# Four quads in a layer's output projection, a shorter sum of weights, and a last norm shared by three engines

## The chip, the cores and the metric

The kernel runs on one core of a Trainium2 chip. The metric is the device time of one execution in microseconds (us); the time before is the median of 3 runs. The engines are named as the profile names them: TensorE (PE; its weight loads are PEld), VectorE (DVE), ScalarE (ACT), GpSimd (POOL) and SyncE (SP), which issues most DMA transfers.

## The reference

A decoder trunk of two layers over 256 tokens with 2048 features, in float32: attention with an output projection, a norm, a gated feed-forward network (FFN) with a short convolution, and a norm again. Cut to what the change touches (layer 2 has `layer == 1`):

```python
for layer in range(DEPTH):                       # 2 layers, x: (1, 256, 2048)
    attn = attention(h, ...)                     # 16 heads of 128; ends with  o @ w_o, (256, 2048) @ (2048, 2048)
    h = layer_norm(ALPHA * h + attn, ln_g[layer, 0], ln_b[layer, 0])
    ffn = conv_ffn(h, ...)                       # ends with  (gelu(g) * v) @ w_down, (256, 5504) @ (5504, 2048)
    h = layer_norm(ALPHA * h + ffn, ln_g[layer, 1], ln_b[layer, 1])

def layer_norm(x, g, b):
    mu, var = mean(x), mean(square(x - mu))
    return (x - mu) * rsqrt(var + 1e-5) * g + b
```

## The kernel before

All weights stream from HBM once, as "halves" of 128x1024 float32 (512 KB). SP loads a half into one of 7 raw buffers (`load_weights`, L115). ScalarE makes its high part, rounded to TensorE's fast float32r format (`high_upto`, L134), and VectorE the remainder (`low_piece`, L143), which frees the raw buffer for the load of the seventh half behind it. A product of a block of weights is three matmuls: high activations by high weights, high by low, low by high (L358 to L360, L566 to L568). The split halves lie in 4 rotating buffers, and, near the changes of stages, in spare "homes" in tiles that are free then (`aside`), with a longer look-ahead (`reach`, set by `settle`).

The order on every engine is written by hand. A call of `take` hands out the next half and records the splits of the halves up to three ahead (`AHEAD`), or as many as `reach` says. `step` ends a half; `at(n, f)` records work of other engines n halves later, `pe_at` that of TensorE.

The projections (`project_out`) have the tokens in two tiles of 128 (t = 0, 1) and the 2048 outputs in four chunks of 512 (c), each of which accumulates over all blocks k of 128 inputs in a bank of PSUM. There are 8 banks, 4 named `acc` and 4 named `at`. In the attention's projection (16 blocks, 32 halves) chunk after chunk is done, both tiles together; at the end of a chunk VectorE folds the bank into the residual `res` (`fold`, L459 or L452) and measures it (`measure`, L464). In the last chunk the last 16 blocks go tile by tile (`tilewise`): all of t = 0, then all of t = 1, so that the norm of the first tile (`moments`, `norm`, L586 to L598) and its transposes (`turn`, L607) run beside the second tile's matmuls. `load_gb` brings gamma and beta.

The FFN's down projection takes two chunks at once (`two_chunks`) and does most of it in "quads": two blocks k by two chunks c by two tiles t, 8 block products, are made with 7, by the Winograd form of Strassen's scheme. For that it needs sums of weights, and sums of activations (`sums`, `four_sums`, `split_sums`). The sums of weights are made in HBM long before their use, by SP's copies and POOL's accumulating DMAs (`sum_weights`, `plan_sums`), and are loaded as halves like the others. Of a quad's blocks 7 are streamed in place of 4. The sums of products are taken apart at the end (`chain`), with banks `a`, `s1`, `s2` and `s3` of kind `at`.

The last norm of the kernel, after layer 2's FFN, is on VectorE: for the second tile it folds the last chunk, measures, finds mean and deviation, and then goes over each of the four chunks twice (L597, L598), each followed by an output transfer on SP (L600).

Of the kernel before, what the change touches and what calls it, by code (L numbers as in the profile page):

```python
# [11 lines left out]
F32 = mybir.dt.float32  # L12
F32R = mybir.dt.float32r
# [30 lines left out]
WARM = 18  # L44
COLS = 2 * (((0, 4), (4, 8), (8, 12), (12, 16)),)
# [6 lines left out]
QUADS = ((10, 8), (10, 8))  # L52
DENSE = ((False, True), (False, False))
LEAD = (4, 2)
S_EARLY = 8
SUMS_AHEAD = (2, 2)
QUAD_ORDER = ((0, 1, 2, 3, 4, 5, 8, 9, 6, 7), (0, 1, 2, 3, 4, 5, 6, 7))
QUAD_LIST = [(l, n, p) for l in range(2) for n in range(2) for p in range(QUADS[l][n])]


def quad_halves(l, n):

    q = QUADS[l][n]
# [10 lines left out]
    return order + [two() for _ in range(len(plain) // 2)]  # L76

# [6 lines left out]
def trunk(ctx: ExitStack, tc: tile.TileContext, wst, wq, xT_in, x_in, relb, onehot, umask, sinks, conv_in, ln_g, ln_b, out):  # L84
# [13 lines left out]
    for l, width in enumerate((4 * D + 2 * DFF, 2 * KVH * P + 2 * D + 2 * DFF)):  # L98
        source += [wst[next(used)] for _ in range(width * D // (P * HW))]
        for n in range(2):  # L100
            source += [tsum[l, n, h[1]][h[2]] if h[0] == "t" else wst[next(used)] for h in quad_halves(l, n)]
# [159 lines left out]
    def sum_weights(q, i):  # L261
# [80 lines left out]
    class Moving:  # L342
# [12 lines left out]
        def mm(self, acc, k, t, wh, wl):  # L355
            sh = self.src(k)[:, t * P:(t + 1) * P]
            sl = self.src(k)[:, T + t * P:T + (t + 1) * P]
            nc.tensor.matmul(acc, sh, wh, start=(k == 0), stop=False)  # L358
# [3 lines left out]
        def tilewise(self, accs, k, n, done):  # L362
# [47 lines left out]

    def scale_shift():
        return [gbp.tile([P, D], F32, name=f"gb{i}") for i in range(2)]

    def project_out(src, nk, li, homes, preload, turnover=None, paired=None, early_sums=None):
# [5 lines left out]
        n_here = sum(len(quad_halves(li // 2, n)) for n in range(2)) if paired is not None else nk * NCH // 2  # L420
# [18 lines left out]
        stats = stat.tile([P, 2, NCH, 6], F32, name="stats", bufs=1, padded_shape=[P, 2, NCH, 10])  # L439
        l = li // 2  # L440
# [13 lines left out]
        ag, rs = {}, {}  # L454

        def fold(n, t, acc, first):
            z = res[:, t, n * 512:(n + 1) * 512]
            if first:
# [7 lines left out]
        def evac(n, t, acc):  # L466
            fold(n, t, acc, paired is None)
            measure(n, t)

        def sums(p):  # L470


            f = paired[:, 0:2 * T].rearrange("p (a b) -> p a b", b=T)

            def whole():
                for i in range(2):
# [595 lines left out]
```

## Time and profile before

| | |
|---|---|
| time, median of 3 runs | 2064.59 us (2064.36 to 2064.78) |
| the profiled execution: its time | 2064.55 us |
| its span, first to last instruction | 2062.8 us |
| granted clock of TensorE, mean | 0.998 |
| busy: TensorE, VectorE, ScalarE, POOL | 2048.8, 1547.9, 1055.3, 118.7 us |
| DMA | 518.37 MB, mean 251 GB/s |

Times in a timeline are from the start of the span. A line of a timeline has the start, the duration, the engine, the line of the kernel, the operation, what it writes and reads, the shape, and, in brackets, the idle time of the engine before it with what ended that. A line of a group has the number of instructions, their busy time and the mean of one in ns. A line of the windows has, for a stretch, the busy time of TensorE, its weight loads, VectorE, ScalarE and POOL, then the granted clock of TensorE, the DMA engines' busy share and what they moved in GB/s. A line of the transfers has their number, their size and the median time from issue to landing.

### The profile page before, as it was taken

The numbers are of one execution on the slowest core, as the hardware profiler recorded it, in microseconds if no ns is written. First come the engines' busy times: TensorE is split into PE (matmuls) and PEld (weight loads), VectorE is DVE, ScalarE is ACT, GpSimd is POOL, SyncE is SP. The second block draws the span as 40 slices with busy tenths as digits, with TensorE's granted clock in tenths as the row PEclk, the third lists the DMA queues.
The fourth block names the chain that finished last, engine by engine and source line by source line (L and its number), as shares of the span: only waits on it lengthen the run. The fifth ranks groups of instructions, "written<-read, shape, count | busy, mean of one in ns | idle before, by whom it ended". The sixth has DMA issues, their size and how long they took to land.

```text
span 2062.8 us, 29246 instructions
## 1 busy us (share of the span) xinstructions
PE 2048.8 (99%) x10968; PEld 1771.4 (86%) x10968; DVE 1547.9 (75%) x2295; ACT 1055.3 (51%) x1470; POOL 118.7 (6%) x130
## 2 busy tenths in 40 slices
PE   9999999999999999999999999999999999999997
PEld 7888888988888888888888888898888888888886
DVE  5555557698887878787786677688887787887767
ACT  5544446344545455565563555445454545556553
POOL 0000000001111111000000000001111111000000
PEclk9999999999999999999999999999999999999999
DMA  9666868379999998688894685639999999769883
GB/s 320 200 207 225 233 226 299 112 245 296 299 294 295 296 266 248 192 281 310 296 326 143 194 244 171 242 118 297 293 292 297 290 303 253 223 205 318 286 301 116
DMA packets 160830, 518.37 MB, mean 251 GB/s; under 512 B 18048, under 2 KB 22720, under 8 KB 159920
## 3 DMA queue, kind: packets, MB, share of 16 engines
q1 hardware_dynamic: 132176, 460.23, 63.1%
q0 software_dynamic: 28224, 56.01, 16.3%
q8 instruction: 86, 1.41, 0.3%
q14 instruction: 56, 0.46, 0.1%
q10 hardware_dynamic: 288, 0.26, 0.0%
HBM read 514.26 MB, written 91.28 MB: 294 GB/s over the span
## 4 chain that ended last, share of the span: by engine, by line
PE 99%; DVE 0%; DMA 0%; ACT 0%; issue 0%
PE acc L305 39%; PE acc L308 20%; PE acc L358 5%; PE acc L359 5%; PE acc L360 5%; PE acc L566 5%; PE acc L568 5%; PE acc L567 5%; PE at L566 2%; PE at L568 2%; PE at L567 2%; PE acc L323 1%; PE acc L335 1%; PE at L693 1%; PE at L726 1%; PE at L719 1%
## 5 line engine op out<-in xcount | busy, mean ns | idle before, releaser
L143 DVE TENSOR_TENSOR wl<-raw,wh 128x1024 fp32r<-128x1024 f32 (+1 forms) x719 | 874.3, 1218 | 421.6 <-ACT wh L134 406.4
L134 ACT ACTIVATE wh<-raw 128x1024 fp32r<-128x1024 f32 (+1 forms) x719 | 758.7, 1057 | 719.1 <-PE acc L305 244.9
L305 PE MATMUL acc<-xT,wh 128*128 128x512 f32 x3456 | 872.7, 394 | 0.0
L305 PEld LDWEIGHTS acc<-xT,wh 128*128 128x128 f32 x3456 | 623.5, 189 | 112.9
L308 PEld LDWEIGHTS acc<-xT,wl 128*128 128x128 f32 x3456 | 471.4, 190 | 33.9
L308 PE MATMUL acc<-xT,wl 128*128 128x256 f32 x3456 | 481.8, 282 | 0.0
L566 PE MATMUL acc<-wh,up 128*128 128x512 f32 x328 | 127.6, 389 | 0.0
L567 PE MATMUL acc<-wl,up 128*128 128x512 f32 x328 | 127.6, 389 | 0.0
L568 PE MATMUL acc<-wh,up 128*128 128x512 f32 x328 | 127.6, 389 | 0.0
L897 DVE SCALAR_TENSOR_TENSOR work<-work,cw 128x255 f32<-128x255 f32 x172 | 83.3, 484 | 6.1
L898 DVE SCALAR_TENSOR_TENSOR work<-work,cw 128x254 f32<-128x254 f32 x172 | 83.2, 484 | 6.2
L896 DVE TENSOR_SCALAR work<-work,cw 128x256 f32<-128x256 f32 x172 | 71.5, 415 | 6.2
L274 POOL DMA_DIRECT2D t<-in_wq_dram x36 | 47.2, 1311 | 469.1 <-DMA t<-in_wq_dram 469.1
L895 DVE TENSOR_TENSOR work<-acc,work 128x256 f32<-128x256 f32 x172 | 71.8, 418 | 1.5 <-ACT work L894 1.5
L568 PEld LDWEIGHTS acc<-wh,up 128*128 128x128 f32 x328 | 61.6, 188 | 12.9
L567 PEld LDWEIGHTS acc<-wl,up 128*128 128x128 f32 x328 | 61.6, 188 | 12.7
L566 PEld LDWEIGHTS acc<-wh,up 128*128 128x128 f32 x328 | 61.6, 188 | 12.6
L894 ACT ACTIVATE work<-acc 128x256 f32<-128x256 f32 x172 | 62.8, 365 | 6.5 <-PE acc L335 6.5
L276 POOL DMA_DIRECT2D t<-t x36 | 37.4, 1039 | 409.1 <-DMA t<-in_wq_dram 372.1
L171 ACT ACTIVATE work<-work 128x256 f32<-128x256 f32 x86 | 36.0, 419 | 47.7 <-DVE work L898 47.6
L358 PE MATMUL acc<-wh,xT 128*128 128x512 f32 x144 | 57.6, 400 | 0.5 <-ACT xT L200 0.5
L359 PE MATMUL acc<-wl,xT 128*128 128x512 f32 x144 | 56.3, 391 | 0.0
(202 smaller groups left out, 2158.6 us busy)
## 6 DMA issues: line engine op xcount, KB each, us to landing
raw<-in_wst_dram SPq DMA_DIRECT2D x703, 512.0 KB, 5.6
t<-in_wq_dram SPq DMA_DIRECT2D x72, 512.0 KB, 8.2
raw<-t SPq DMA_DIRECT2D x72, 512.0 KB, 4.6
t<-in_wq_dram POOLq DMA_DIRECT2D x36, 512.0 KB, 12.7
t<-t POOLq DMA_DIRECT2D x36, 512.0 KB, 10.1
t<-in_wq_dram POOLq DMA_DIRECT2D x36, 256.0 KB, 7.5
band<-ud SPq DMA_DIRECT2D x4, 512.0 KB
bias<-band SPq DMA_DIRECT2D x4, 512.0 KB, 4.3
```

The lines of the kernel that those rows point to most:

```text
L134: nc.scalar.activation(wh[:, c], raws[s][:, c], AF.Copy)
L143: nc.vector.tensor_tensor(out=wl[:, c], in0=raws[s][:, c], in1=wh[:, c].bitcast(F32), op=ALU.subtract)
L305: nc.tensor.matmul(acc, cols(wh, j), xT[:, k, :], start=(k == 0), stop=False)
L308: nc.tensor.matmul(o, cols(wl, j), xT[:, k, 0:T], start=False, stop=(k == KB - 1))
L358: nc.tensor.matmul(acc, sh, wh, start=(k == 0), stop=False)
L359: nc.tensor.matmul(acc, sh, wl, start=False, stop=False)
L360: nc.tensor.matmul(acc, sl, wh, start=False, stop=(k == self.nk - 1))
L566: nc.tensor.matmul(bank(key), a[0], wh[:, c], start=key not in begun, stop=False)
L567: nc.tensor.matmul(bank(key), a[0], wl[:, c], start=False, stop=False)
L568: nc.tensor.matmul(bank(key), a[1], wh[:, c], start=False, stop=stop)
L897: nc.vector.scalar_tensor_tensor(c[:, 1:T], h[:, 0:T - 1], w[:, 1:2], c[:, 1:T], op0=ALU.mult, op1=ALU.add)
L898: nc.vector.scalar_tensor_tensor(c[:, 2:T], h[:, 0:T - 2], w[:, 0:1], c[:, 2:T], op0=ALU.mult, op1=ALU.add)
```

## The change

1. Layer 2's output projection (`QUADS` has a third number for each layer, 0 and 4) makes its first two chunks together in `two_chunks`, with four quads over blocks 0 to 7 and plain products over 8 to 15. `wo_halves` gives the order of its 22 halves: five plain ones, fifteen with the quads' blocks and sums among them, two plain ones. The sums of activations are made during the attention, after every second of the first eight heads (`sum_heads`), into the tiles that hold gamma and beta later; so those are loaded in eight pieces by SP once the quads are done. `turnover` and `settle` come after 8 halves as before. The chunks 2 and 3 are as they were.
2. `sum_weights`: the third transfer in POOL's chain adds to one 512-column block (256 KB) and not to two, and the last one adds the third sum, t[1][:, 0:512], and not a block of weights. `plan_sums` makes four sums early in each layer's attention, from half 54 and half 2, where it made two, from half 64 and half 16.
3. The last norm. In the second tile the last four blocks (`ENDING`) go in two halves of 256 columns, and the first one is folded and measured while the second runs, in a bank of its own. The first three chunks of the tile are multiplied by gamma ahead of the end (`scaled`). When mean m and reciprocal deviation r are known, the term b - m r g is made on TensorE, as a product of the columns (-m r, 1), transposed, with the rows (g, b); ScalarE multiplies the three chunks by r, and VectorE adds the two. Twelve transposes (`STILL`) run on TensorE while it would be idle. The last chunk is done as before, and the third is put out in two pieces. The preload of a table for Exp after the last root is left out.

```diff
-QUADS = ((10, 8), (10, 8))
+QUADS = ((10, 8, 0), (10, 8, 4))
+WO_LEAD = [(k, 0) for k in range(8, 14)] + [(k, 1) for k in range(8, 12)]
+WO_LAST = [(k, c) for c in range(2) for k in (14, 15)]
...
+def wo_halves(l):
+    q = range(QUADS[l][2])
+    mid = [b for p in q for b in ((2 * p, 0), (2 * p + 1, 0), (2 * p + 1, 1))]
+    mid[3:3] = [(12, 1)]
+    mid[10:10] = [(13, 1)]
+    halves = lambda bs: [("w", *bs[i:i + 2]) for i in range(0, len(bs), 2)]
+    order = halves(WO_LEAD)
+    sums, others = [("t", p, i) for p in q for i in range(2)], halves(mid)
+    while sums:
+        order += [sums.pop(0)] + others[:1]
+        others = others[1:]
+    return order + others + halves(WO_LAST)
...
         if i == 3:
-            nc.gpsimd.dma_start(half(1), twice(t[0][:, 0:512]), accum_op=ALU.add)
+            nc.gpsimd.dma_start(t[1][:, 0:512], t[0][:, 0:512], accum_op=ALU.add)
         if i == 4:
-            nc.gpsimd.dma_start(t[1][:, 512:], wq[j][:, 1, :], accum_op=ALU.add)
+            nc.gpsimd.dma_start(t[1][:, 512:], t[1][:, 0:512], accum_op=ALU.add)
...
-                    self.mm(accs[t], k + i, t, *blocks[i])
+                    if not (t and ending and i >= n - ENDING):
+                        self.mm(accs[t], k + i, t, *blocks[i])
+                    elif i == n - 1:
+                        for c in (slice(0, 256), slice(256, 512)):
+                            for m in range(n - ENDING, n):
+                                self.mm(accs[t + c.start // 256][:, 0:256], k + m, t, *(w[:, c] for w in blocks[m]),
+                                        first=k + n - ENDING if c.start else 0)
+                            if c.start == 0:
+                                ending()
...
+        def last_piece(i):
+            z = res[:, 1, (NCH - 1) * 512:]
+            if i == 0:
+                add(z, accs[1], z)
+            else:
+                add(z[:, 256:], accs[2][:, 0:256], z[:, 256:])
+            nc.vector.bn_stats(stats[:, 1, NCH - 1 + i, :], z[:, i * 256:(i + 1) * 256])
+
+        def finish():
+            nc.vector.tensor_scalar(mr[:, 0:1], ag[1][:, 0:1], rs[1], -1.0, op0=ALU.mult, op1=ALU.mult)
+            mrT = wpool.tile([P, HW], F32, name="raw")[0:2, 0:P]
+            still = acc_tile()
+            for _ in range(STILL):
+                nc.tensor.transpose(still[:, 0:P], ident, ident)
+            pt = psum.tile([P, 512], F32, name="at")
+            nc.tensor.transpose(pt[0:2, 0:P], mr, ident)
+            part = lambda n: res[:, 1, n * 512:(n + 1) * 512]
+            by_rs = lambda n: nc.scalar.activation(part(n), part(n), AF.Copy, scale=rs[1])
+            by_rs(0)
+            nc.scalar.activation(mrT, pt[0:2, 0:P], AF.Copy)
+            shift = []
+            for n in range(NCH - 1):
+                shift.append(psum.tile([P, 512], F32, name="at"))
+                nc.tensor.matmul(shift[n], mrT, paired[0:2, n * 512:(n + 1) * 512], start=True, stop=True)
+            norm(1, COLS[1][-1])
+            for n in range(NCH - 1):
+                if n:
+                    by_rs(n)
+                for c in (slice(0, 512),) if n < NCH - 2 else (slice(0, 256), slice(256, 512)):
+                    z = part(n)[:, c]
+                    add(z, shift[n][:, c], z)
+                    nc.sync.dma_start(out[P:2 * P, n * 512:(n + 1) * 512][:, c], z)
...
                 for c in COLS[0]:
                     norm(0, c)
+                if not after:
+                    rows()
+                    for n in range(NCH - 1):
+                        scaled(n)
...
         gb = scale_shift()
-        load_gb()
-        for n in range(NCH):
+        if QUADS[l][2]:
+            quads_end = max(i for i, h in enumerate(quad_halves(l, 2)) if h[0] == "t" or h[1][0] < 2 * QUADS[l][2])
+            for i in range(2 * NCH):
+                at(quads_end + AHEAD + 1 + i, load_gb_piece, i // 2, i % 2)
+            accs = two_chunks(0, 2, lambda: turnover.work.rearrange("p a b -> p (a b)"), {8: (turnover, settle)})
+            for t in range(2):
+                at(4, evac, 1, t, accs[t])
+        else:
+            load_gb()
+        for n in range(2 if QUADS[l][2] else 0, NCH):
...
-        plan_sums([q for q in QUAD_LIST if q[0] == l][:SUMS_AHEAD[l]], (64, 16)[l], 10)
+        wo = [(1, 2, p) for p in range(QUADS[1][2])]
+        plan_sums(wo[2 * l:2 * l + 2] + [(l, 0, p) for p in range(2)], (54, 2)[l], 10)
...
+        def sum_heads(h):
+            p = h // 2
+            if h % 2 == 0 or p >= QUADS[l][2]:
+                return
+            if not places:
+                places.extend(gbp.tile([P, D], F32R, name=f"gb{i}") for i in range(2))
+            w = pool.tile([P, 2 * T + 512], F32, name="fs", bufs=1)
+            for i, step in enumerate(pair_sums(lambda i: oT[:, 2 * p + i, :], w[:, 0:2 * T], w[:, 2 * T:], *wo_sums(p))):
+                at(6 + i, step)
```

`pair_sums` holds what `sums` did: `whole` adds high and low parts, `combine` makes the four sums, `split` splits them. `rows` loads gamma and beta of three chunks as two rows, on POOL's queue.

More of the change, by code (lines that the diff above doesn't have):

```diff
@@ L454, in project_out, with fold @@
         ag, rs = {}, {}
-        def fold(n, t, acc, first):
+        if not after:
+            mr = stat.tile([P, 2], F32, name="mr", bufs=1)
+        def fold(n, t, acc):
             z = res[:, t, n * 512:(n + 1) * 512]
-            if first:
+            if (n, t) not in opened:
+                opened.add((n, t))
                 nc.vector.scalar_tensor_tensor(z, z, ALPHA, acc, op0=ALU.mult, op1=ALU.add)
@@ L551, in chain @@
                     at(m, combine_banks, w[i], banks[name], w[j], op)
-                    at(m + later, fold, n + c, t, w[0 if name == "s2" else i], c > 0 or not ready)
+                    at(m + later, fold, n + c, t, w[0 if name == "s2" else i])
             def combine_banks(o, a, b, op):
@@ L585, in moments @@
             ag[t] = stat.tile([P, 2], F32, name="ag")
[L586 removed]
+            nc.vector.bn_aggr(ag[t], stats[:, t, 0:NCH if after or not t else NCH + 1, :])
             sd = stat.tile([P, 1], F32, name="sd")
             nc.scalar.activation(sd, ag[t][:, 1:2], AF.Sqrt, bias=eps, scale=1.0)
[L589 removed]
+            if t and after:
                 nc.scalar.activation(junk, eps, preload)
@@ L636, in late @@
                 if not after:
-                    for c in COLS[1]:
-                        norm(1, c)
+                    finish()
         if paired is not None:
```

142 lines of the change are left out of this document (93 added, 49 removed).

## The prediction

> **What bounds the kernel now.** I read the page first (busy time, then the chain that ended last), then the timeline of the two stretches that are edited, then the landing times.
>
> ```profile
> span 2062.8 us, 29246 instructions
> PE 2048.8 (99%) x10968; PEld 1771.4 (86%) x10968; DVE 1547.9 (75%) x2295; ACT 1055.3 (51%) x1470; POOL 118.7 (6%) x130
> PE 99%; DVE 0%; DMA 0%; ACT 0%; issue 0%
> ```
>
> TensorE is busy for all but 14.0 us of the span, and the chain is TensorE throughout. So only three things can move the time: matmuls that go, matmuls that newly wait, and what stands after the last matmul. The profiled execution took 2064.55 us, 1.75 us more than its span and 0.04 us under the median of 2064.59; differences worked out in the trace are applied to that median.
>
> ```profile
> 2047.78 0.39 PE L358 MATMUL acc<-wh,up 128*128 128x512 f32 x1
> 2050.27 0.39 PE L360 MATMUL acc<-wh,up 128*128 128x512 f32 x1
> 1252.17 1.11 PE L308 MATMUL acc<-xT,wl 128*128 128x256 f32 x8
> 1249.89 0.60 PE L693 MATMUL at<-kT,qT 128*128 128x256 f32 x2
> ...
> 2047.10 0.75 DVE L598 SCALAR_TENSOR_TENSOR res<-res,rs,gb 128x512 f32<-128x512 f32 x1
> 2050.70 0.69 DVE L452 TENSOR_TENSOR res<-acc,res 128x512 f32<-128x512 f32 x1 [2.85 <-PE acc L360]
> 2051.43 0.69 DVE L464 BATCH_NORM_STATS2 stats<-res 128x6 f32<-128x512 f32 x1
> 2052.15 0.26 DVE L586 BATCH_NORM_AGGREGATE ag<-stats 128x2 f32<-128x24 f32 x1
> 2052.45 0.29 ACT L588 ACTIVATE sd<-ag,eps 128x1 f32<-128x1 f32 x1 [10.58 <-DVE ag L586]
> 2052.78 0.16 DVE L635 RECIPROCAL rs<-sd 128x1 f32<-128x1 f32 x1 [0.36 <-ACT sd L588]
> 2052.86 0.73 DVE L597 SCALAR_TENSOR_TENSOR res<-res,ag,gb 128x512 f32<-128x512 f32 x1
> 2053.63 0.75 DVE L598 SCALAR_TENSOR_TENSOR res<-res,rs,gb 128x512 f32<-128x512 f32 x1
> ...
> 2057.98 0.75 DVE L598 SCALAR_TENSOR_TENSOR res<-res,rs,gb 128x512 f32<-128x512 f32 x1
> ```
>
> The durations of matmuls contain their pipeline's latency; what counts is from start to start. The first two rows are the first and the last of the final 12 matmuls: 2.49/11 = 0.2264 us for each 512 columns. Eight matmuls of 256 columns in 1.11 us, with 0.28 of latency in it, stand (1.11 - 0.28)/7 = 0.119 us apart: half width costs half, plus 5%. The row of L693 is one plain f32 matmul in two passes, 0.22 us apart for 256 columns (0.60 less the last one's 0.38). The rest is the tail: VectorE alone from 2050.70 to 2058.73, eight operations of the norm being 5.9 us of it.
>
> **The quads, on TensorE.** A quad replaces 8 block products by 7, each of 3 matmuls. Four quads: 4 x 3 = 12 matmuls of 512 columns, 12 x 0.2264 = **-2.72 us**. No TensorE instruction is added in that stretch.
>
> **The quads, what they ask of the others.** Their sums of activations fall into the attention before it: for a pair of heads two additions of 256 columns, four operations of 128 and one of 512 on VectorE, one copy of 512 on ScalarE, as the FFN's late quads do them.
>
> ```profile
> L478 DVE TENSOR_TENSOR work<-up 128x256 f32<-128x256 f32 x4 | 1.5, 418 | 0.0
> L400 DVE TENSOR_TENSOR work<-work 128x128 f32<-128x128 f32 x6 | 1.6, 287 | 0.1
> L400 DVE TENSOR_TENSOR gb<-work,gb 128x512 fp32r<-128x512 f32 x2 | 1.4, 685 | 0.0
> ...
> 1150.00:1200.00 50.00, 50.00 (x297) 44.46 (x296) 38.40 (x91) 28.79 (x68) 2.99 (x3) 1.00 0.69 201
> ```
>
> That is 2 x 0.42 + 4 x 0.29 + 0.69 = 2.7 us of VectorE per pair, 10.7 us for four. VectorE is idle 11.6 of 50 us there, 23%. The weight products alone of those eight heads take 16 halves x 8 x (0.2264 + 0.119) = 44 us, with 10.2 us of idle time: level. But the sums have no date before the projection, and a split made late has three halves of TensorE work ahead of its use: cost 0, up to 1 us if that cover is thin.
>
> The first two chunks go from 16 halves to 22: 14 raw and 8 of sums. Call them 0 to 21, and 22 the first of the third chunk. Five lead halves have 12 matmuls, the next fifteen (8 of sums among them) have 6 or 9, the last two 12. Every half is still split by ScalarE and VectorE, so a split now has 1.36 us of TensorE beside it in place of 2.72.
>
> ```profile
> 1273.51 1.06 ACT L134 ACTIVATE wh<-raw 128x1024 fp32r<-128x1024 f32 x1 [2.02 <-PE acc L360]
> 1274.61 1.23 DVE L143 TENSOR_TENSOR wl<-raw,wh 128x1024 fp32r<-128x1024 f32 x1 [1.79 <-ACT wh L134]
> 1280.04 3.89 ACT L134 ACTIVATE up<-raw 128x1024 fp32r<-128x1024 f32 x4
> 1284.51 4.62 DVE L143 TENSOR_TENSOR up<-raw,up 128x1024 fp32r<-128x1024 f32 x4
> 1278.47 0.68 DVE L459 SCALAR_TENSOR_TENSOR res<-res,acc 128x512 f32<-128x512 f32 x1
> ```
>
> From a buffer's release to its next split is 1.10 us of ScalarE and 1.23 of VectorE, 2.3 us; the shortest three halves take 3 x 6 x 0.2264 = 4.1 us, so no quad half comes late. The tight place is the end. The third chunk reuses the banks of the first one's accumulators, and the two folds that empty them stand in VectorE's queue behind the split of half 27, in the order of the built program, because the look-ahead into the spare homes starts at half 13. Splits 9 to 15 are paced by TensorE (split 15 waits for half 11), 16 to 27 by nothing. Back to back a split takes VectorE (4.62 - 1.23)/3 = 1.13 us and ScalarE (3.89 - 1.06)/3 = 0.94. After half 11 ends: 1.10 + 13 x 1.13 + 0.68 = 16.5 us to the first fold's end. TensorE takes 75 matmuls (halves 12 to 21), 17.0 us, before it needs that bank, and the second one three matmuls later. Margin 0.5 us: cost **0**, if the raw halves arrive.
>
> ```profile
> raw<-in_wst_dram SPq DMA_DIRECT2D x12, 512.0 KB, 5.9
> raw<-in_wst_dram SPq DMA_DIRECT2D x19, 512.0 KB, 7.5
> t<-in_wq_dram POOLq DMA_DIRECT2D x3, 512.0 KB, 13.2
> ...
> 1285.00:1290.00 5.00, 5.00 (x24) 4.14 (x23) 5.00 (x5) 2.13 (x2) 0.00 (x0) 1.00 0.96 308
> 1290.00:1295.00 5.00, 5.00 (x24) 4.14 (x23) 4.88 (x5) 4.25 (x4) 0.00 (x0) 1.00 1.02 407
> ```
>
> Seven raw buffers make a loop: issue to landing 5.9 us (the median from 1282 to 1300, when today's burst of splits runs), ScalarE 1.06, VectorE 1.23, in all 8.2 us for seven splits, against 7 x 1.13 = 7.9. In 12 splits that loses 12/7 x 0.3 = 0.5 us, just the margin. From 505 to 560, while sums of weights run (the third row is one kind of their transfers), the median is 7.5 us.
>
> After that VectorE has 6 more splits (6.8 us), four combinations of banks and four more folds (8 x 0.68 = 5.4 us) before the first tile's norm.
>
> ```profile
> 1300.03 0.69 DVE L459 SCALAR_TENSOR_TENSOR res<-res,acc 128x512 f32<-128x512 f32 x1 [5.16 <-PE acc L360]
> 1321.79 0.69 DVE L459 SCALAR_TENSOR_TENSOR res<-res,acc 128x512 f32<-128x512 f32 x1 [2.44 <-PE acc L360]
> 1333.35 0.69 DVE L459 SCALAR_TENSOR_TENSOR res<-res,acc 128x512 f32<-128x512 f32 x1 [6.57 <-PE acc L360]
> ```
>
> It idles 14.2 us there now; 12.2 more work and 2.7 us less time leave it level with TensorE, with the idle time of the lead halves (such as the 1.79 us ahead of the split at 1274.61) as the reserve. Cost 0; VectorE is the next bound of this stretch.
>
> **The sums of weights and the queues.** Per quad one accumulation by POOL shrinks from 512 to 256 KB, and the last reads the third sum in place of the weights; both were already one after the other. Four quads are added, and the other early ones start 10 or 6 halves later, on SP (two copies each) and POOL (three). In layer 2's attention two of POOL's four bias loads now stand behind a wait for a sum; the heads that need them come more than ten halves later. The gamma and beta of that norm go from two POOL transfers to eight SP transfers 23 to 30 halves in, behind loads that wait longer than they do. The rows of gamma and beta for the tail are two small POOL transfers with nothing behind them. No matmul in the trace waits for any of these, so all of it is 0, within +-0.2.
>
> **The end.** The last four blocks go in two column halves: 24 matmuls of 256 columns. Last start 2047.78 + 23 x 0.119 = 2050.52 in the old clock, end 2050.80 against 2050.66: **+0.14**. VectorE meanwhile finishes the first tile's norm at 2047.8, then clears a small tile, scales three chunks (0.6 each, a little over half of a split's pace), folds the last chunk and measures its first half, to 2050.8: just in time. Then, each from the old gaps with 0.27 off for 256 columns: addition 2050.84, statistics 2051.30, aggregate 2051.75, root 2052.05, reciprocal 2052.38, product of mean and reciprocal 2052.58 to 2052.78. Now the new relay.
>
> ```profile
> L607 PEld LDWEIGHTS at<-ident,res x16: 138/141/143, 1338.4 to 1344.3; 128*128 128x128 f32 x16
> L607 PE MATMUL at<-ident,res x16: 270/272/273, 1338.6 to 1344.4; 128*128 128x128 f32 x16
> ```
>
> TensorE transposes two columns (weights 0.14, matmul 0.27, 0.05 to be released) to 2053.24, ScalarE copies (as the root's 0.29) to 2053.55, TensorE makes three f32 products of 512 columns. By L693 each is 2 x 0.44 = 0.87 us, so they are ready at 2053.55 + 0.19 + 0.87 + 0.17 = 2054.78, 2055.65 and 2056.52. ScalarE's scaling by the reciprocal (three of 0.6 us, a little over half of a 1.06 split, from 2052.6) and VectorE's last chunk (2052.8 to 2054.2) are done before. VectorE adds the last product in two halves: 2056.56 and 2056.91, end 2057.33. Before, it was 2058.73: **-1.40 us** with the +0.14 in it. The table load at L590 goes, off the path.
>
> ```profile
> L600 SPq DMA_DIRECT2D out_dram<-res x8: 332/332/344, 2043.5 to 2058.8; - x8
> DMA to landing us min/median/max: 2.4/2.5/2.5
> ```
>
> The last output transfer is 128 KB in place of 256: between 0 and, if the 2.5 us were half data, -0.6; the one before it is issued 0.33 us earlier on the same engines. I take **-0.2**, nearer to no change, as these times hardly vary.
>
> **Sum:** -2.72 - 1.40 - 0.20 = -4.3 us, 2064.59 - 4.3 = **2060.3 us**. About 0.2%, 4.1 us, is what a measurement of this kernel tells from no change: the forecast lies at that border, and terms of 0.2 us decide the side.
>
> **The rivals.** *A, the relay is not the bound.* If the f32 products ran in half the time, VectorE's own work would set the end: 2054.2 + 2 x 0.62 + 0.35 + 0.42 = 2056.2, 1.1 us earlier: 2059.2. Against it: the two passes of L693. *B, the first two chunks stall.* With landings of 7.5 us the loop loses 12/7 x (7.5 + 2.29 - 7.9) = 3.2 us, less the margin of 0.5: +2.7, 2063.0; half of it at 6.7 us. For it: the 308 GB/s in a stretch where the engines were 96% busy. Against it: no sums run there, and 407 GB/s right behind. This includes the case that the quads do not do what they say in time, 12 matmuls gone and a stall as long. *C, the clock falls in the relay.*
>
> ```profile
> 2053.00:2055.00 2.00, 0.00 (x0) 0.00 (x0) 1.96 (x3) 1.25 (x2) 0.00 (x0) 1.00 0.00 0
> 2055.00:2057.00 2.00, 0.00 (x0) 0.00 (x0) 1.93 (x4) 0.00 (x0) 0.00 (x0) 0.74 0.49 190
> ```
>
> The granted clock fell to half at 2057 - 2 x 0.26/0.5 = 2055.96, 5.3 us after the last matmul. If the 12 added transposes do not hold it, it falls 5.3 us after 2050.80, at 2056.1, and the last 0.4 us of products take twice as long: +0.4, 2060.7; if it falls right behind the first product, two take twice: +1.7, 2062.0. Against it: work on TensorE until about 2052.1. The Trainium skill (TensorE: Matmul & The Clock Gate, Part 4) states that transposes do not count as busy for this gate, and by its window of 3.4 us (Part 1) the clock could fall at 2054.2, an estimate of 2062.6 us. The trace's one fall came later than that window, and no run here has transposes alone. *D, slower.* The same loop at the change of chunks: a landing time L costs 12/7 x (L - 5.6) - 0.5, which eats up the 4.3 us at L = 8.4 and is 0.2% slower than before from L = 10.8. At 11 us it is +8.8: 2069.1. Of the rows above only POOL's accumulations take that long, and none of them runs there.
>
> **How the numbers follow.** Forecast 0.57 (two thirds of it past 4.1 us, since terms bounded to some +-0.5 us lie around 4.3), A 0.12, B 0.16, C 0.11, D 0.04. Faster by over 0.2%: 0.38 + 0.12 = 0.50; within: 0.19 + 0.16 + 0.11 = 0.46; slower: 0.04, all of D. The range goes down to A, 2059.2, and up to B with landings of 7.0 us (+1.9), which takes in C: 2062.2. Outside lie D, the worse half of B and the far side of A, less than 0.2.
>
> **What would show it.** Right: four fewer products in layer 2's projection (180 matmuls where 192 were), no idle before the first matmul of its third chunk, and TensorE's last 512-column matmul 2.7 us earlier. In the tail the three products 0.87 us apart, VectorE's last additions waiting on TensorE, and its last end 6.5 us after the last matmul of the weights. Wrong: a TensorE gap at the third chunk with VectorE behind on splits (B, D), a granted clock of 0.5 before the products end (C), products 0.44 apart (A), or VectorE later than 2050.8 at the last fold.

## The result, and the profile after

| | before | after |
|---|---|---|
| time, median of 18 runs each | 2064.53 us (2064.05 to 2064.87) | 2060.84 us (2060.05 to 2062.13) |
| ratio | | 0.9983, 95% interval 0.9976 to 0.9990 |
| the profiled execution: time, span | 2064.55, 2062.8 us | 2062.13, 2060.3 us |

The change takes 3.7 us, just under 0.2%: less than the 4.3 us that were forecast. A ratio of 1, no change, lies outside the interval. The times after lie in two groups, eleven from 2060.05 to 2060.87 and seven from 2061.46 to 2062.13; before, all 18 lie within 0.9 us. The profiled execution is the slowest of the 18, so it shows what goes wrong and not the usual case.

The page after: TensorE is now idle for 7.8 us of the span, where it was 14.0, and the chain is still its own.

```profile
span 2060.3 us, 29412 instructions
PE 2052.5 (100%) x10987; PEld 1772.3 (86%) x10987; DVE 1568.3 (76%) x2342; ACT 1064.7 (52%) x1483; POOL 121.4 (6%) x142
PE 99%; DVE 0%; DMA 0%; ACT 0%; issue 0%
```

TensorE's busy time went up, although 12 matmuls went: the tail's products and transposes are in it. The timeline of the place where the third chunk of layer 2's projection begins (start, duration, engine, line, and the idle time before it with what ended that):

```profile
1284.02 3.49 DVE L171 TENSOR_TENSOR xT<-raw,xT 128x1024 fp32r<-128x1024 f32 x3
1287.43 4.70 DVE L171 TENSOR_TENSOR up<-raw,up 128x1024 fp32r<-128x1024 f32 x4
1292.27 5.06 DVE L171 TENSOR_TENSOR wl<-raw,wh 128x1024 fp32r<-128x1024 f32 x4
1297.25 1.28 DVE L521 SCALAR_TENSOR_TENSOR res<-res,acc 128x512 f32<-128x512 f32 x2
...
1293.74 1.06 ACT L162 ACTIVATE wh<-raw 128x1024 fp32r<-128x1024 f32 x1 [0.22 <-DMA raw<-in_wst_dram]
1295.01 1.06 ACT L162 ACTIVATE wh<-raw 128x1024 fp32r<-128x1024 f32 x1 [0.21 <-DMA raw<-in_wst_dram]
...
1297.22 0.39 PE L617 MATMUL acc<-up,st 128*128 128x512 f32 x1
1298.08 0.47 PE L386 MATMUL acc<-up,st 128*128 128x512 f32 x1 [0.47 <-DVE res L521]
```

From 1297.22 to 1298.08 is 0.86 us where 0.23 is usual: **0.63 us lost**. TensorE waits for the fold, the fold stands behind the split of half 27, and ScalarE's part of each split waits for a transfer, the last of them 1.27 us apart. The windows of the same stretch (busy time of PE, PEld, DVE, ACT, POOL, then granted clock, the DMA engines' share, GB/s):

```profile
1280.00:1285.00 5.00, 5.00 (x24) 4.14 (x23) 4.73 (x5) 4.70 (x6) 0.00 (x0) 1.00 1.00 324
1290.00:1295.00 5.00, 5.00 (x24) 4.14 (x23) 4.74 (x5) 4.05 (x4) 0.00 (x0) 1.00 1.03 414
```

The loads issued from 1276 to 1298, before and after (number, size, median us from issue to landing):

```profile
raw<-in_wst_dram SPq DMA_DIRECT2D x14, 512.0 KB, 5.8
raw<-in_wst_dram SPq DMA_DIRECT2D x16, 512.0 KB, 6.2
```

The tail, from the last matmul of the weights:

```profile
2048.21 0.28 PE L388 MATMUL acc<-wh,up 128*128 128x256 f32 x1
2048.33 1.47 PE L679 MATMUL acc<-ident 128*128 128x128 f32 x12
2048.53 0.42 DVE L511 TENSOR_TENSOR res<-acc,res 128x256 f32<-128x256 f32 x1
2050.11 0.16 DVE L739 RECIPROCAL rs<-sd 128x1 f32<-128x1 f32 x1 [0.36 <-ACT sd L637]
2050.57 0.27 PE L681 MATMUL at<-ident,mr 128*2 128x128 f32 x1 [0.77 <-DVE mr L675]
2051.26 4.52 PE L689 MATMUL at<-work,raw 2*128 2x512 f32 x6 [0.41 <-ACT raw L685]
2052.42 0.69 DVE L511 TENSOR_TENSOR res<-at,res 128x512 f32<-128x512 f32 x1 [0.45 <-PE at L689]
2054.18 0.69 DVE L511 TENSOR_TENSOR res<-at,res 128x512 f32<-128x512 f32 x1 [1.07 <-PE at L689]
2055.89 0.76 DVE L511 TENSOR_TENSOR res<-at,res 128x256 f32<-128x256 f32 x2 [1.01 <-PE at L689]
```

And three windows of 1 us in it:

```profile
2051.00:2052.00 1.00, 0.74 (x2) 0.48 (x3) 0.93 (x2) 0.96 (x4) 0.00 (x0) 1.00 0.03 8
2052.00:2053.00 1.00, 1.00 (x2) 0.28 (x1) 0.58 (x1) 0.58 (x1) 0.00 (x0) 0.64 0.16 63
2053.00:2054.00 1.00, 1.00 (x3) 0.46 (x2) 0.11 (x1) 0.00 (x0) 0.00 (x0) 0.50 0.54 211
```

The relay is built as forecast, and VectorE waits for each product. But the granted clock falls to half at 2052.28, at the beginning of the second of three products, and the six passes, which take 2.84 us with the clock up (experiment 3), take 4.52. VectorE ends 8.43 us after the start of the last matmul of the weights; before, that was 8.45 us. In this execution the tail gains nothing up to VectorE's end: rival C, at its full price. From there to the span's end it is 3.7 us, where it was 4.1.

So there were three questions: are the quads worth 2.72 us where nothing stalls; is the stall of 0.6 us the pace of the loads or a slip of mine; and what decides, from run to run, whether the clock falls among the products.

### The profile page after: what moved, and what is told of

Same layout as the page of the kernel before. It is cut to its first block, busy times and chain, and to the rows that moved or that the text cites. A ratio compares the mean times of both kernels' runs of the same rounds, so it can differ in the third digit from the quotient of the medians.

```text
span 2060.3 us, 29412 instructions
## 1 busy us (share of the span) xinstructions
PE 2052.5 (100%) x10987; PEld 1772.3 (86%) x10987; DVE 1568.3 (76%) x2342; ACT 1064.7 (52%) x1483; POOL 121.4 (6%) x142
## 4 chain that ended last, share of the span: by engine, by line
PE 99%; DMA 0%; DVE 0%; ACT 0%; issue 0%; DVEq 0%; ACTq 0%
PE acc L333 39%; PE acc L336 20%; PE acc L617 5%; PE acc L615 5%; PE acc L616 5%; PE acc L386 5%; PE acc L388 5%; PE acc L387 5%; PE at L617 2%; PE at L615 2%; PE at L616 2%; PE acc L351 1%; PE acc L363 1%; PE at L806 1%; PE at L839 1%; PE at L704 1%
## 5 line engine op out<-in xcount | busy, mean ns | idle before, releaser
L304 POOL DMA_DIRECT2D t<-t x40 | 32.9, 824 | 433.0 <-DMA t<-in_wq_dram 389.5
L386 PE MATMUL acc<-wh,xT 128*128 128x512 f32 x144 | 57.6, 400 | 0.2 <-ACT xT L228 0.2
L388 PE MATMUL acc<-wh,xT 128*128 128x512 f32 x144 | 56.4, 392 | 0.0
```

What stands on the lines that cost most here:

```text
L386: nc.tensor.matmul(acc, sh, wh, start=(k == first), stop=False)
L388: nc.tensor.matmul(acc, sl, wh, start=False, stop=(k == self.nk - 1))
```

## The experiments

My theory: the quads and the tail are worth what was forecast, and two losses were left out, the stall at the third chunk and the fall of the clock in a part of the runs. The rival: terms were mis-sized, or a wait appears elsewhere. Times are medians of 11 runs (9 in experiment 10), beside runs of the kernel before on the same chip (medians 2064.38, 2064.43 and 2064.43 us for the three groups of four).

**1. The quads and sums, with the old tail.**

```diff
-                if not after:
-                    rows()
-                    for n in range(NCH - 1):
-                        scaled(n)
...
-                    finish()
+                    for c in COLS[1]:
+                        norm(1, c)
...
-            mv.tilewise(accs, nk - WINDOW_BLOCKS, WINDOW_BLOCKS, late, None if after else lambda: last_piece(0))
+            mv.tilewise(accs, nk - WINDOW_BLOCKS, WINDOW_BLOCKS, late)
```

> The quads and the sums of weights as changed, the end of the kernel as before. Theory: the quads take 12 matmuls, 2.72 us, and give 0.63 us back in a stall at the third chunk's first matmul, where the two folds stand behind splits that wait for loads; so 2062.4 us, 2.1 below before, and the runs lie within some 0.8 us as those of before do, because the spread of the changed kernel comes from its end. Rival: the stall changes from run to run and makes the spread; then these runs spread over 1.5 us or more as well.

Measured: 2061.84 us (2061.50 to 2062.59), 2.5 under before where I expected 2.1, ratio 0.9989 (0.9980 to 0.9998). The stall is there, with 0.46 us lost. One group, within 1.1 us: the rival, a spread that the stall makes, falls.

**2. The new tail, without quads.**

```diff
-QUADS = ((10, 8, 0), (10, 8, 4))
+QUADS = ((10, 8, 0), (10, 8, 0))
...
-        plan_sums(wo[2 * l:2 * l + 2] + [(l, 0, p) for p in range(2)], (54, 2)[l], 10)
+        plan_sums(wo[2 * l:2 * l + 2] + [(l, 0, p) for p in range(2)], (64, 16)[l], 10)
```

> The new end and the shorter sums, no quads in the projection. Theory: the end alone is worth 1.4 to 2.0 us while the clock holds and up to 1.7 us less where it falls during the three f32 products; so about 2062.8 us, with runs in two groups some 1 us apart, and with the run without the end (the quads only) it adds up to the changed kernel's 2060.8. Rival: the end gains nothing and all of the 3.7 us is the quads': 2064.5.

Measured: 2063.51 us, ratio 0.9995 (0.9986 to 1.0003): three runs at 2062.08 to 2062.20, eight at 2063.36 to 2064.05. No stall at the third chunk. The two groups belong to the tail alone. The median is 0.7 us over the 2062.8 that I expected, since so many runs lie in the upper group; with experiment 1 it adds up to 3.4 us of the change's 3.7.

**3. The change with a slower look-ahead**, so that fewer splits stand ahead of the two folds.

```diff
-                reach[i] = i + min(AHEAD + (i - first) * 3 // 5, len(ring) - 1)
+                rate = 2 if QUADS[l][2] and paired is None else 3
+                reach[i] = i + min(AHEAD + (i - first) * rate // 5, len(ring) - 1)
```

> As changed, but the look-ahead into the spare homes of layer 2's projection grows by 2 halves in 5 and not by 3 in 5, so that at the end of half 20 two splits fewer stand before the folds. Theory: the stall of 0.63 us goes, 2060.2 us, and nothing else moves. Rival: the folds are not what the third chunk waits for, or VectorE then comes late at the first tile's norm: 2060.8 or more.

Measured: 2060.32 us, ratio 0.9980 (0.9971 to 0.9989); nine of eleven runs at 2059.60 to 2060.44, the other two at 2061.91 and 2062.74. The folds come 2.6 us earlier and TensorE goes over into the third chunk without a pause (timeline of this kernel):

```profile
1294.67 1.27 DVE L522 SCALAR_TENSOR_TENSOR res<-res,acc 128x512 f32<-128x512 f32 x2
...
1297.12 0.39 PE L618 MATMUL acc<-up,st 128*128 128x512 f32 x1
1297.35 0.39 PE L386 MATMUL acc<-up,st 128*128 128x512 f32 x1
...
2047.36 0.28 PE L388 MATMUL acc<-wh,up 128*128 128x256 f32 x1
2050.41 2.84 PE L690 MATMUL at<-work,raw 2*128 2x512 f32 x6 [0.41 <-ACT raw L686]
2053.36 0.76 DVE L512 TENSOR_TENSOR res<-at,res 128x256 f32<-128x256 f32 x2 [0.17 <-PE at L690]
```

In its profiled execution the clock held through the products, and VectorE ended 6.75 us after the start of the last matmul of the weights.

**4. Nine products of 512 columns in place of the twelve transposes**; their result is not used.

```diff
-STILL = 12
+STILL = 9
...
-                nc.tensor.transpose(still[:, 0:P], ident, ident)
+                nc.tensor.matmul(still, src(nk - 1)[:, P:T], fill[0], start=True, stop=True)
```

> As changed, but 9 float32r matmuls of 512 columns with the last weights stand in place of the 12 transposes (their output is not used). Theory: transposes do not hold the clock; real matmuls until 2050.4 of the old trace's clock put off its fall by 2 us or more, beyond the three products, which then stand 0.87 us apart in every run: 2060.0 us and a spread under 0.8 us. Rival: the fall comes from the idle gaps of the relay, whatever runs before: runs spread over 2 us as now, 2060.8 us.

Measured: 2060.73 us (2060.35 to 2061.84), ratio 0.9983 (0.9974 to 0.9992). Ten of eleven within 0.9 us, the stall still there. The median did not fall to 2060.0 as I expected.

**5 and 6. No filler at all, and the change again beside it.**

```diff
-STILL = 12
+STILL = 0
```

> The change without its twelve transposes; nothing else differs, so the clock's windows begin where they do in the change. So far TensorE's clock, once the dense work ends, has fallen at a multiple of 3.413 us after its first rise, and in the change about 7 of 18 times fell among the three products, which cost some 1.4 to 1.7 us. Theory 1, the transposes count for the clock at least in part: without them a window needs its dense work from the last weights alone, the fall comes 1 to 1.5 us of phase earlier, and it meets the products in three runs of four or more. Most times then lie at 2061.5 to 2062.5, median about 2061.8, and in the profiled run the last two or three products take 0.85 us a pass. Theory 2, transposes do not count: the same two groups in about the same shares as the change, median 2060.8, and in the profiled run the fall lies where the grid puts it, 3.8 to 5.3 us after the last matmul of the weights.

> The changed kernel itself, run beside the others for its shares of the two groups: 2060.8, some 60% of the times at 2060.0 to 2060.9 with warm products and 40% at 2061.4 to 2062.2 with cold ones. If the groups belonged to the chip that ran it and not to the phase of the clock, all its times would lie in one of them.

Measured: without filler 2062.19 us (2060.92 to 2063.70), eight of eleven at 2061.8 or more, ratio 0.9990 (0.9981 to 0.9999); the change again 2060.98 us (2060.50 to 2062.57), eight of eleven at 2061.24 or less, ratio 0.9984 (0.9976 to 0.9993). So the transposes do hold the clock, in part of the runs, and are worth 1.2 us; the two groups are not the chip's, since the change again has both on this one. In the profiled execution of the change again the clock held, and VectorE's end came 6.75 us after the last matmul of the weights.

**7. Both repairs: the slower look-ahead and the nine products.** The edits of 3 and 4 together.

> The change with both repairs: the look-ahead into the spare homes two steps in five instead of three, and in place of the twelve transposes nine 512-column float32r products whose result is not used. If the two losses are the stall at the third chunk (0.6 us) and the fall of the clock among the products (1.7 us in a part of the runs), both are gone: 2059.7 to 2060.0, spread under 1 us, no idle time of over 0.3 us ahead of the third chunk. If the look-ahead run was only luckier in the clock, this one gives the same 2060.3 and the dense filler adds nothing to it.

Measured: 2060.42 us (2059.82 to 2061.23), where I expected 2060.0 at most, ratio 0.9980 (0.9972 to 0.9989). The stall is gone, but the profiled execution, the slowest of them, has the clock fall at 2052.88, in the second product. The nine products were no safe cure: what was my error about the clock?

Every profiled execution answers. The clock first rises 4.25 to 6.79 us after the start of the span and stays up for 2044.58, 2048.00 or 2051.41 us: 599, 600 or 601 times 3.4133 us. So in all fourteen traces it changes only at the marks of a grid, and the grid begins elsewhere in every run. The windows between the marks around the fall, of the kernel before, of experiments 1, 3, 7 and 11 (the last is below), each cut at that run's own marks:

```profile
2049.14:2052.56 3.42, 1.52 (x7) 0.94 (x5) 1.65 (x3) 0.11 (x1) 0.00 (x0) 1.00 0.07 26
2052.56:2055.97 3.41, 0.00 (x0) 0.00 (x0) 3.12 (x6) 1.67 (x3) 0.00 (x0) 1.00 0.20 77
2055.97:2059.30 3.33, 0.00 (x0) 0.00 (x0) 2.69 (x4) 0.00 (x0) 0.00 (x0) 0.50 0.41 157
```

```profile
2047.26:2050.68 3.42, 0.81 (x4) 0.35 (x2) 2.14 (x5) 0.80 (x2) 0.00 (x0) 1.00 0.00 0
2050.68:2054.09 3.41, 0.00 (x0) 0.00 (x0) 3.31 (x6) 0.98 (x2) 0.00 (x0) 0.50 0.21 79
```

```profile
2047.22:2050.63 3.41, 2.22 (x18) 1.79 (x17) 2.78 (x8) 1.47 (x4) 0.00 (x0) 1.00 0.00 0
2050.63:2054.04 3.41, 2.62 (x6) 0.81 (x5) 2.55 (x5) 0.95 (x2) 0.00 (x0) 1.00 0.39 154
2054.04:2057.40 3.36, 0.00 (x0) 0.00 (x0) 0.07 (x1) 0.00 (x0) 0.00 (x0) 0.50 0.45 159
```

```profile
2049.47:2052.88 3.41, 2.98 (x10) 1.50 (x10) 2.52 (x6) 2.42 (x5) 0.00 (x0) 1.00 0.01 4
2052.88:2056.20 3.32, 2.35 (x3) 0.33 (x1) 1.70 (x4) 0.00 (x0) 0.00 (x0) 0.50 0.61 236
```

```profile
2048.93:2052.35 3.42, 1.27 (x6) 0.73 (x4) 1.68 (x4) 0.34 (x2) 0.00 (x0) 1.00 0.00 1
2052.35:2055.70 3.35, 0.00 (x0) 0.00 (x0) 3.28 (x6) 1.44 (x2) 0.00 (x0) 0.50 0.20 78
```

A fall comes at the end of a window that held too little, so what is in the window ahead of each fall, and in the last one that was passed, tells what counts. Passed: 1.52 us of matmuls of the weights (before); 0.27 of those with 1.74 of transposes and 0.22 of the tail's products (experiment 3, 2.22 in all). Failed: 0.81 us of weights (experiment 1); 1.27 us of weights (11); 2.62 us of the tail's products and nothing else (3); 1.12 of full products, 0.27 of transposes and 1.6 of the tail's (7, 2.98 in all). So for matmuls of the weights the limit lies between 1.27 and 1.52 us of 3.41. Transposes must then count for more than half as much as these, (1.27 - 0.27)/1.74 = 0.57 at the least, or experiment 3's first window would have failed. And the tail's products, float32 with 2 rows of weights, count for little: under a fifth, or experiment 7's 1.6 us of them would have lifted its window over the limit. The nine products of experiment 7 ended at 2050.59, 1.12 us into their window: too early. The runs without a trace have a mean granted clock beside their time, and it is the lower the earlier the fall: in experiment 2 it is 0.999 in the three fast runs and 0.998 in the eight others, and in the change 0.998 in six of the upper seven and in one of the lower eleven. So the two groups are those of the clock.

**8. The same products with 128 rows.** Experiment 3 with 126 rows of zeros added to the weights, and ones against them.

```diff
+            nc.gpsimd.memset(paired[:, 0:(NCH - 1) * 512], 1.0)
...
+            nc.gpsimd.memset(wide[0], 0.0)
...
-            mrT = wpool.tile([P, HW], F32, name="raw")[0:2, 0:P]
+            mrT = wpool.tile([P, HW], F32, name="raw")[:, 0:P]
...
-                nc.tensor.matmul(shift[n], mrT, paired[0:2, n * 512:(n + 1) * 512], start=True, stop=True)
+                nc.tensor.matmul(shift[n], mrT, paired[:, n * 512:(n + 1) * 512], start=True, stop=True)
```

> The change with the slower look-ahead, and its three float32 products made with 128 rows in place of 2: the 126 added rows have zeros on the side of the weights and ones on the other, so the result is the same, and so is the number of passes and columns. So far windows of 3.413 us that held 2.6 us of these two-row products and nothing else ended in a fall of the clock, where 1.5 us of ordinary matmuls held it. Theory 1, the clock counts rows in use: full rows hold it, the window that holds the products passes, the fall comes 3.4 us later than it did in the same phase, all products are 0.43 us a pass, and no time lies over 2060.6. Theory 2, it counts what the rows carry (zeros against ones is little), or not this kind of pass at all: the fall comes at the end of the first window with less than 1.4 us of weights and transposes, as before; times as those of the look-ahead alone, 2060.3 with a few at 2061.5 to 2062.7.

Measured: 2060.37 us, all eleven from 2059.71 to 2060.70 (two over the 2060.6 of theory 1), ratio 0.9980 (0.9971 to 0.9989). Its windows, and under them the one ahead of the fall in experiment 4:

```profile
2049.16:2052.57 3.41, 2.32 (x6) 1.20 (x7) 2.48 (x5) 2.23 (x5) 0.00 (x0) 1.00 0.17 68
2052.57:2055.99 3.42, 0.82 (x2) 0.00 (x0) 1.45 (x3) 0.00 (x0) 0.00 (x0) 1.00 0.66 237
2055.99:2058.00 2.01, 0.00 (x0) 0.00 (x0) 0.00 (x0) 0.00 (x0) 0.00 (x0) 0.50 0.03 7
...
2051.11:2054.53 3.42, 2.99 (x8) 1.11 (x7) 2.69 (x5) 2.07 (x4) 0.00 (x0) 1.00 0.21 79
```

The first of them held 0.30 us of transpose and 2.02 us of these products, no weights, and was passed. Experiment 4's held 0.09 us of full products, 0.27 of transpose and 2.63 of the products with 2 rows, more in all, and was failed. Theory 1 holds: the same kind of pass keeps the clock up with 128 rows and not with 2, even where 126 rows are zeros. No run lies in an upper group; as experiment 3 had only two of eleven there, it is the windows that show this, not the count.

**9. The products in float32r, one pass each.** Experiment 3 with the rows of gamma and beta and the columns (-m r, 1) rounded to float32r by ScalarE, so that term is less exact.

```diff
+            nc.scalar.activation(gbr, paired[0:2, 0:(NCH - 1) * 512], AF.Copy)
...
-            mrT = wpool.tile([P, HW], F32, name="raw")[0:2, 0:P]
+            mrT = spool.tile([P, HW], F32R, name="wh")[0:2, 0:P]
...
-                nc.tensor.matmul(shift[n], mrT, paired[0:2, n * 512:(n + 1) * 512], start=True, stop=True)
+                nc.tensor.matmul(shift[n], mrT, gbr[:, n * 512:(n + 1) * 512], start=True, stop=True)
```

> The change with the slower look-ahead of the earlier run and with the three products of the tail in float32r, one pass each, in place of float32 in two: the rows of gamma and beta and the pair of columns are rounded to float32r by ScalarE, so the term b - m r g is less exact. If the three float32 products set the end (0.87 us apart, as the change's trace has them), they now come 0.23 us apart, VectorE's own additions set the end, and the tail shortens by about 1.0 us: 2059.3 where the slower look-ahead alone gave 2060.3 and where its best runs gave 2059.6, so 2058.6 in the best. It should also hardly depend on the clock any more, since the last product ends less than 3.5 us after the last matmul of the weights: the spread of its times under 0.8 us. If something else sets the end (ScalarE's scaling by the reciprocal deviation, VectorE's last chunk), the gain is under 0.3 us and VectorE's last additions do not wait.

Measured: 2059.56 us (2059.11 to 2060.21, one at 2062.08 that I can't explain), ratio 0.9978 (0.9969 to 0.9987); I expected 2059.3 and a spread under 0.8. The timeline: three products in 0.94 us, VectorE's four additions without a pause, and SP's issues of the output behind them.

```profile
2051.39 0.94 PE L693 MATMUL at<-st,wh 2*128 2x512 f32 x3 [0.42 <-ACT wh L689]
2052.01 1.95 DVE L512 TENSOR_TENSOR res<-at,res 128x512 f32<-128x512 f32 x4
2052.72 2.17 SPq L701 DMA_DIRECT2D out_dram<-res  x4
```

VectorE ends 5.62 us after the last matmul of the weights, 1.13 earlier than with float32 products: they were the bound. But from there to the span's end it is 4.48 us in place of 3.72, so 0.76 of it is given back.

**10. The last two output transfers on ScalarE's queue.**

```diff
-                    nc.sync.dma_start(out[P:2 * P, n * 512:(n + 1) * 512][:, c], z)
+                    q = nc.scalar if n == NCH - 2 else nc.sync
+                    q.dma_start(out[P:2 * P, n * 512:(n + 1) * 512][:, c], z)
```

> The kernel with float32r products, with its last two output transfers (the third chunk in two pieces) issued by ScalarE, which is idle then, in place of SP. In that kernel VectorE ended at 2053.95, and SP issued the last transfer only at 2054.49, since it took 0.33 to 0.40 us for each of five and had a gap of 0.41 before the fourth. If SP's issuing is the end there, the last transfer is now issued about 0.4 us earlier and lands as long after as before: 0.4 us less, 2059.2. If the transfers themselves are the end (the same engines move them, 2.8 us from issue to landing), the time stays at 2059.6.

Measured: 2059.45 us (2059.06 to 2059.81), ratio 0.9976 (0.9966 to 0.9985), the fastest kernel here, by no more than the runs differ. The transfers of the last 12 us (issues: queue, number, size, median us to landing):

```profile
out_dram<-res SPq DMA_DIRECT2D x3, 256.0 KB, 2.6
out_dram<-res ACTq DMA_DIRECT2D x2, 128.0 KB, 3.3
```

The last issue came 0.14 us after VectorE's end in place of 0.54, but the landing took 3.3 us in place of 2.9: the span still ends 4.49 us after VectorE. SP's issuing was not the bound. It is probably the last megabyte of output, which leaves at 240 to 390 GB/s through DMA engines that are busy until about 2055, 2.3 us before the span's end; no run tests this.

**11. The sums of weights alone, in the kernel before.**

```diff
-            nc.gpsimd.dma_start(half(1), twice(t[0][:, 0:512]), accum_op=ALU.add)
+            nc.gpsimd.dma_start(t[1][:, 0:512], t[0][:, 0:512], accum_op=ALU.add)
...
-            nc.gpsimd.dma_start(t[1][:, 512:], wq[j][:, 1, :], accum_op=ALU.add)
+            nc.gpsimd.dma_start(t[1][:, 512:], t[1][:, 0:512], accum_op=ALU.add)
```

> The kernel before with the second part alone: POOL's third accumulation over 256 KB in place of 512, and the last reading the third sum. If nothing on the critical path waits for these transfers, 2064.4, no change within 0.3 us. If the sums of weights were late anywhere, a gain of 0.5 us or more would show here, and part of the change's gain would be theirs.

Measured: 2064.37 us, ratio 1.0001 (0.9992 to 1.0010). Nothing waits for them.

**12. Quads and sums, old tail, slower look-ahead.** The edits of 1 and 3 together.

> The four quads and the sums with the old tail, and the look-ahead into the spare homes two steps in five. If a quad is worth its three matmuls and the stall at the third chunk is the only thing that it costs, the time is that of before less 12 x 0.2264: 2061.7, and 0.5 us under the quads with the old look-ahead (2061.84 when that was run, 2.5 under its kernel before). If the stall is made good later anyway (by a wait at the first norm, or by the shift of everything behind it), both look-aheads give the same, 2.5 us under before.

Measured: 2061.48 us (2061.09 to 2061.87), 2.95 under before (2.5 in experiment 1, with the stall), ratio 0.9985 (0.9977 to 0.9994); no stall.

The spans begin with up to 1 us of difference (the first matmul of the weights starts 4.99 to 6.15 us in), so the quads are best read inside the traces, from the first matmul of layer 2's projection to the last matmul of the weights, starts in us:

| | stall | no stall |
|---|---|---|
| old tail, no quads (before; experiment 11) | | 796.90; 796.90 |
| old tail, quads (1; 12) | 794.67 | 794.11 |
| new tail, no quads (2) | | 797.09 |
| new tail, quads (after, again, 4, 5; 3, 7, 8, 9, 10) | 795.12, 794.74, 795.11, 795.06 | 794.37 four times, 794.44 (8) |

## Why the prediction was right, and where it was not

**The quads, -2.72.** Right: 797.09 - 794.37 = 2.72 with the new tail, 796.90 - 794.11 = 2.79 with the old one. What they ask of VectorE in the attention is hidden as stated: from the first matmul of the weights to the projection it is 1247.80 us before and 1247.90 after.

**What they cost, 0.** Wrong, and this is the step that failed: the price of the loop of raw buffers. It was reckoned from a landing time of 5.9 us, that of the kernel before, to lose 0.5 us in 12 splits, "just the margin". But the pace of 1.13 us that I gave to the splits needs 0.524 MB / 1.13 us = 464 GB/s, and the prediction's own row of 1290 to 1295 has the DMA engines full (1.02) at 407. After, they move 414, that is 1.27 us a half, and the landing grows with the pace: 6.2 us where the same stretch had 5.8 before, and 6.4 in the prediction's own window, 1282 to 1300. With 6.2 the prediction's loop gives 12/7 x (6.2 - 5.6) = 1.0 us, 0.5 over the margin: the formula was good and the landing put into it was not. VectorE's splits show the loss: the four from 1287.43 take 4.84 us to the next and of the four from 1292.27 three take 5.06 - 1.23 = 3.83, together 0.76 us over 1.13 each. The margin of 0.5 and 0.63 more are gone, 1.13 in all; the other 0.4 stands at the two ends, which the prediction put at nothing: ScalarE begins split 15 at 1280.65, 0.20 us after TensorE went over to half 12, and TensorE goes on 0.15 us after the fold's end at 1297.93. It is rival B in kind. In the table the stall costs 0.37 to 0.75 us. Experiment 3 shows that the place of the folds behind the splits makes a stall of it: its loads of 1276 to 1298 land as late (6.2 us), fewer splits stand ahead of the folds, and the stall is gone.

**The sums and queues, 0 +-0.2.** Right for the shorter sums (experiment 11). The added sums have no run of their own; that nothing waits for them rests on the 1247.80 and 1247.90 us above.

**The end, -1.40.** Right where the clock holds: 6.75 us from the start of the last matmul of the weights to VectorE's end, against 2057.33 - 2050.52 = 6.81 forecast and 8.45 before; the last start is 0.19 later (797.09 against 796.90; 0.25 forecast), in all -1.51. The two-pass products are the bound, so rival A fell; its price of 1.1 us for products in half the time was what experiment 9 measured on VectorE, though the output gives most of it back. **The landing, -0.2**: from VectorE's end to the span's end 4.05 us before, 3.72 and 3.95 after where the clock held. But the old tail has 3.79 and 3.82 too in experiments 12 and 1, so this isn't shown to be the smaller transfer.

**Rival C** was priced rightly and given too little chance. 8.43 - 6.75 = 1.68 us at VectorE's end is its "up to +1.7"; in the times the medians of the two groups lie 0.8 us apart in the change and 1.5 in experiment 2. I had one fall to go by, 5.3 us after the last matmul, and took that for a delay. It isn't one: the fall lies on the grid of 3.413 us, and how far behind the work it comes depends on where the grid began, which differs from run to run. Against the chance of 0.11, ten of 29 runs of the change lie in the upper group, about a third. The Trainium skill (TensorE: Matmul & The Clock Gate, Part 1) has this rule: a window of 3413 ns that runs free and doesn't begin with the kernel; all traces here agree, with 599, 600 or 601 windows between rise and fall. The Trainium skill (TensorE: Matmul & The Clock Gate, Part 4) says that the full clock doesn't engage for transposes, which do not count as busy in the same way. No run here tests them on raising the clock, but for holding it this is not borne out with float32 transposes: with 0.27 us of weights and 1.74 us of transposes a window was passed, with 1.27 us of weights alone it was failed, and without the transposes the median was 1.2 us higher.

**The sum.** Without the stall the change gives 4.06 us (experiment 3, with two runs of eleven in the upper group, and experiment 8 with none), against 4.3 forecast. The stall and the runs whose clock falls in the tail bring it to 3.7, which is under 4.1 and so within 0.2%: a forecast that stood 0.2 us past this border was, as the prediction said, settled by terms of that size. The time lies in the range because the two large terms were right and the range had room for both losses.

## What to carry to other kernels

Where a burst of loads is planned, divide its bytes by its pace and hold that against the GB/s that a full DMA row of the same trace shows; a loop of latencies sees that bound only with the landing time of the faster pace. Where a tail leaves TensorE idle and then uses it again, work out from the marks of the clock's grid what each window will hold, for every place the grid can begin, and fill the window with work on all rows, or make the late work short enough not to matter. Where the runs of a change split into two groups, look for what differs between them in the traces before the median is believed; here it was the clock.

## What the runs showed of the hardware that was not expected

Whether work holds TensorE's granted clock depends on the rows in use: a window of 3.41 us with 2.63 us of products with 2 rows and 0.27 us of transpose let it fall, one with 2.02 us of the same products with 128 rows, 126 of them zeros, and 0.30 us of transpose held it. Only 2 and 128 rows were tried. The limit, for matmuls of the weights alone, lies between 1.27 and 1.52 us of the window, 37 to 45%. And a window in which TensorE was busy for 2.99 of 3.41 us, as the profile counts it, was not busy enough.
